# One more round between the residual and the second product of the Newton step, and three more instructions that the modulation sums stand behind

## The chip, the cores and the metric

The kernel runs on one core of one Trainium2 chip. The metric is device time in microseconds (us) of one execution. A core has TensorE (PE in the rows; PEld are its weight loads), VectorE (DVE), ScalarE (ACT), GpSimd (POOL) and SyncE (SP, which here issues nearly all DMAs). Each engine takes its instructions in the order in which they stand in the program, and waits for the others by semaphores.

## The reference

One layer of a diffusion backbone over 256 context and 256 latent tokens, model width 2048. What matters here is the RWKV-7 part, 16 heads of width 64, in both directions of time, first over the context, then over the latent tokens:

```python
def wkv_scan(r, w, k, v, kk, a, s0, reverse):
    def step(s, inp):
        r_t, w_t, k_t, v_t, kk_t, a_t = inp
        sa = jnp.einsum('bhij,bhj->bhi', s, -kk_t)
        s = (s * w_t[:, :, None, :] + sa[..., None] * (kk_t * a_t)[:, :, None, :]
             + v_t[..., None] * k_t[:, :, None, :])
        return s, jnp.einsum('bhij,bhj->bhi', s, r_t)
...
yx_rw, _ = rwkv_mix(rwkv_streams(conv3(px[..., :RW_COLS], rw_shift[i]), *rw_args), s_ctx, *out_args)
yx = jnp.concatenate([yx_rw.astype(px.dtype), short_conv_mix(px, conv_w[i], grid_conv3),
                      fourier_mix(px)], axis=-1) @ w_out[i]
x = x + ga1 * yx
x = x + ga2 * ffn(modulate(rms_norm(x, norm_ffn[i]), sh2, sc2), w_gate[i], w_up[i], w_down[i])
```

The modulation vectors (`ga1`, `sh2`, `sc2`, `ga2`) are sums over 2048 rows of a weight matrix, weighted by `silu(c)`.

## The kernel before

The program has three stages. The first makes the modulated inputs and a part of the projections. The second, the recurrence, holds everything between the projections and the FFN, and the third is the FFN.

**The recurrence** handles 16 states one after another: state 0 to 7 are the eight pairs of heads over the context, 8 to 15 the same pairs over the latent tokens. The tokens of a state are cut into 4 chunks of 64. Four kinds of Python generators work on a state: `rw_prep` makes its operands, two `rw_inverse` (one for each direction of time) invert the 64 by 64 triangular matrices of the chunks, and `rw_scan` runs over the chunks. `recurrence()` goes round by round: in every round each live generator emits its instructions up to its next `yield`, and yields an estimate of the TensorE time of what it emitted. A second stream, `fillers()`, holds all other TensorE work of this stage (projections, the Fourier part, the first part of the output projection). After the generators of a round, `tick` draws fillers until their estimates reach what is left of the round's budget: 2.2 (context) or 2.1 (latent) less what the generators have yielded, at least 0.65. TensorE's order is this order of the code (`manual_schedule`). The other engines' orders are made by a list scheduler when the program is built.

The fillers stop at two places. The second of three groups of the output projection waits until the first four pairs of heads are normed, and from its 9th column block on (`HOLD`) until the last state is done.

**The inverse** (`rw_inverse`) takes a mask step (`de`), five doubling steps in 16 bits (`sx`, `de`), and then one Newton step in 32 bits: a first product (TensorE, `iv<-d,ga`), the residual (VectorE, `idm`, one buffer for both directions), a second product (TensorE, `iv<-e,idm`), and the sum that refines the inverse (VectorE, `e`).

**The modulation sums** (`modvecs`) are 192 VectorE instructions of 128x512 (`macc<-wm`), each on a weight block that has just been loaded. 0.9 of them are drawn per round. `issue_after(self.lastv.ins)` places a sum behind the instruction that `lastv` names on VectorE, which is set in the doubling steps and in the scan.

Of the kernel before, what the change touches and what calls it, by code (L numbers as in the profile page):

```python
# [14 lines left out]
ALU = mybir.AluOpType  # L15
# [185 lines left out]
class Builder:  # L201
# [26 lines left out]
    def cst(self, name, i=0, n=None, rows=slice(0, P)):  # L228
        s, e = CC.at[name]
        return self.consts[rows, s + i:(e if n is None else s + i + n)]  # L230
# [503 lines left out]
    def rw_inverse(self, st, d):  # L734

        nc, mp, cst = self.nc, self.mp, self.cst
        V, S, G, T = nc.vector, nc.scalar, nc.gpsimd, self.t
        while len(st["GA"]) <= d or self.inverted[d] < st["n"]:
            yield 0.0
        ga = st["GA"][d]  # L740
        msk = lambda l: self.bc4(self.m16[:, 6 * d + l])
        quads = [(c, h) for c in range(NC) for h in range(2)]

        im = T(mp, [P, NC, C], F16, f"im{d}")
        for h in range(2):
            (G, V)[h].tensor_tensor(im[HV[h]], ga[h][HV[h]], self.bc4(cst("i64", rows=HV[h])), op=ALU.add)  # L746
        for h in range(2):
            G.tensor_tensor(ga[h][HV[h]], ga[h][HV[h]], self.bc4(cst("i64", rows=HV[h])), op=ALU.add)
        yield 0.0
        pq = T(self.iv, [P, NC, C], F32, f"iv{d}")  # L750
        for c, h in quads:
            self.mm(pq[HV[h], c], im[HV[h], c], self.i16[HV[h]], True, True)

        xe = T(mp, [P, 2, NC, C], F16, f"de{d}")
        V.tensor_tensor(xe[:, 0], pq, msk(0), op=ALU.mult)
        V.tensor_tensor(xe[:, 1], im, self.bc4(self.m16[:, 12 + d]), op=ALU.mult)
        yield 0.12
        sx = T(mp, [P, NC, C], F16, f"sx{d}")
        for l in range(1, 6):
            pd = T(self.iv, [P, 2, NC, C], F32, f"iv{d}")  # L760
            for c, h in quads:
                self.mm(pd[HV[h], 0, c], im[HV[h], c], xe[HV[h], 0, c], True, True)
            self.lastv = V.tensor_tensor(sx, pd[:, 0], msk(l), op=ALU.mult)
            yield 0.12
            for c, h in quads:
                self.mm(pd[HV[h], 1, c], sx[HV[h], c], xe[HV[h], 1, c], True, True)
            for c, h in quads:
                self.mm(pd[HV[h], 0, c], xe[HV[h], 1, c], sx[HV[h], c], True, True)
            if l < 5:
                S.copy(xe, pd)  # L770
            else:
                d32 = T(mp, [P, NC, C], F32, "d32")
                e32 = T(mp, [P, NC, C], F32, f"e32{d}", 2)
                S.copy(d32, pd[:, 0])
                S.copy(e32, pd[:, 1])
            yield 0.34
        pr = T(self.iv, [P, 2, NC, C], F32, f"iv{d}")
        for c, h in quads:
            self.mm(pr[HV[h], 0, c], ga[h][HV[h], c], d32[HV[h], c], True, True)
        r = T(mp, [P, NC, C], F32, "idm")  # L780
        V.tensor_tensor(r, self.bc4(cst("i64")), pr[:, 0], op=ALU.subtract)
        yield 0.6
        for c, h in quads:
            self.mm(pr[HV[h], 1, c], r[HV[h], c], e32[HV[h], c], True, True)
        V.tensor_tensor(e32, e32, pr[:, 1], op=ALU.add)
        st["E"][d] = e32
        self.inverted[d] += 1
        yield 0.6

    def rw_scan(self, st):  # L790

# [455 lines left out]
```

## Time and profile before

| | |
|---|---|
| time, three runs | 1812.42, 1812.53, 1805.78 us (median 1812.42) |
| profiled execution: time | 1805.89 us |
| profiled execution: span from first to last instruction | 1804.1 us |
| mean granted TensorE clock | 0.976 of full speed |
| recurrence in this execution | about 232 to 1036 us |
| TensorE / VectorE busy in the span | 94% / 58% |

Busy time is the time in which an engine has an instruction under way. Matmuls overlap, so that eight of them listed with 0.28 us each can take 0.12 us each from start to start. The span is the profiled execution from its first to its last instruction; the execution's own time is 1.8 us longer.

### The profile page before, as it was taken

To read this page: it belongs to the slowest core of one execution; us is meant where nothing else is said; L and a number is where in the kernel's file an instruction comes from. 1 tells how busy PE (TensorE), PEld (TensorE's weight loads), DVE (VectorE), ACT (ScalarE), POOL (GpSimd) and SP (SyncE) were. 2 spreads that over 40 slices of the span, in tenths; PEclk is the share of its full clock that TensorE was granted. 3 is DMA by queue.
4 is the path that set the end of the run, shared out by engine and by line. 5 is a ranking of instruction groups with operands and counts; after the bars stand their busy time and mean duration, and the time that the engine had idled before them with its cause. 6 is when DMAs were issued, how large, how long until landed. Compare 5 with 4: busy or idle time off the path is not lost.

```text
span 1804.1 us, 47455 instructions
## 1 busy us (share of the span) xinstructions
PE 1698.8 (94%) x19960; PEld 1561.3 (87%) x19960; DVE 1053.4 (58%) x1851; ACT 828.0 (46%) x1577; POOL 747.2 (41%) x650
## 2 busy tenths in 40 slices
PE   7999999988999899899988979999999999999996
PEld 3888988887888787787876779999999999999996
DVE  4444357777678777768875697555555444333333
ACT  2223455555655555444553444444444444444442
POOL 1224454455666554455652452232322323323332
PEclk9999999999999999899998989999999999999998
DMA  9992233455455443544542257777777566665654
GB/s 359 344 332 87 87 103 120 143 157 155 155 164 164 143 141 115 158 129 121 155 124 60 80 165 245 240 242 234 237 230 231 188 200 188 191 190 184 189 185 136
DMA packets 139237, 318.92 MB, mean 177 GB/s; under 512 B 14224, under 2 KB 40464, under 8 KB 139024
## 3 DMA queue, kind: packets, MB, share of 16 engines
q1 hardware_dynamic: 137936, 314.84, 54.5%
q8 instruction: 156, 2.56, 0.6%
q10 hardware_dynamic: 1088, 1.05, 0.2%
q14 instruction: 57, 0.47, 0.1%
HBM read 313.74 MB, written 2.10 MB: 175 GB/s over the span
## 4 chain that ended last, share of the span: by engine, by line
PE 77%; DVE 13%; ACT 4%; issue 3%; DMA 2%; POOL 1%; SPq 0%; DVEq 0%; ACTq 0%; POOLq 0%
PE gu L233 25%; PE pj L233 17%; PE dn L233 13%; PE pacc L233 4%; PE pp L233 4%; PE iv L233 4%; PE st L233 3%; PE acc L233 3%; DVE macc L1096 3%; PE pmod L233 2%; DVE bk L645 1%; DVE XL L1184 1%; DMA wm<-wma 1%; DVE im L746 1%; DVE HL L1155 1%
## 5 line engine op out<-in xcount | busy, mean ns | idle before, releaser
L269 POOL TENSOR_TENSOR wlo<-w,whi 128x512 fp32r<-128x512 f32 (+2 forms) x309 | 517.0, 1676 | 747.7 <-ACT whi L266 724.1
L266 ACT CAST whi<-w 128x1024 fp32r<-128x1024 f32 (+2 forms) x472 | 401.3, 851 | 552.5 <-PE gu L233 200.9
L233 PE MATMUL gu<-XH,whi 128*128 128x256 f32 (+1 forms) x1408 | 392.9, 279 | 4.5 <-ACT whi L266 4.0
L233 PE MATMUL gu<-XH,wlo 128*128 128x256 f32 (+1 forms) x1408 | 391.3, 279 | 2.1 <-POOL wlo L269 1.3
L269 DVE TENSOR_TENSOR wlo<-w,whi 128x1024 fp32r<-128x1024 f32 (+1 forms) x175 | 205.7, 1176 | 312.4 <-ACT whi L266 312.4
L233 PE MATMUL gu<-XL,whi 128*128 128x256 f32 x1344 | 372.6, 278 | 0.1
L233 PE MATMUL pj<-XH,whi 128*128 128x256 f32 x1016 | 290.1, 314 | 3.1 <-DVE XL L1028 2.3
L233 PEld LDWEIGHTS gu<-XH,whi 128*128 128x128 f32 x1408 | 266.1, 189 | 5.8 <-ACT whi L266 4.8
L233 PEld LDWEIGHTS gu<-XH,wlo 128*128 128x128 f32 x1408 | 265.5, 189 | 2.8 <-POOL wlo L269 1.7
L233 PE MATMUL pj<-XL,whi 128*128 128x256 f32 x1016 | 259.6, 284 | 0.6 <-DVE XL L269 0.6
L233 PE MATMUL pj<-XH,wlo 128*128 128x256 f32 x1016 | 259.6, 284 | 0.0
L233 PEld LDWEIGHTS gu<-XL,whi 128*128 128x128 f32 x1344 | 253.9, 189 | 0.3 <-DVE XL L1184 0.3
L233 PEld LDWEIGHTS pj<-XH,whi 128*128 128x128 f32 x1016 | 183.1, 192 | 18.3 <-issue 1.8
L233 PE MATMUL dn<-HL,whi 128*128 128x256 f32 x704 | 196.0, 278 | 0.0
L233 PE MATMUL dn<-HH,wlo 128*128 128x256 f32 x704 | 194.4, 276 | 0.0
L233 PE MATMUL dn<-HH,whi 128*128 128x256 f32 x704 | 194.3, 276 | 0.0
L233 PEld LDWEIGHTS pj<-XL,whi 128*128 128x128 f32 x1016 | 183.8, 193 | 2.4 <-issue 0.9
L233 PEld LDWEIGHTS pj<-XH,wlo 128*128 128x128 f32 x1016 | 183.0, 193 | 2.6 <-POOL whi L268 1.7
L1096 DVE SCALAR_TENSOR_TENSOR macc<-wm,sc,macc 128x512 f32<-128x512 f32 x180 | 164.6, 914 | 1.8 <-DMA wm<-wmb 1.1
L233 PEld LDWEIGHTS dn<-HL,whi 128*128 128x128 f32 x704 | 132.1, 188 | 1.4
L233 PEld LDWEIGHTS dn<-HH,wlo 128*128 128x128 f32 x704 | 132.2, 188 | 0.0
L233 PEld LDWEIGHTS dn<-HH,whi 128*128 128x128 f32 x704 | 132.1, 188 | 0.0
(302 smaller groups left out, 2774.4 us busy)
## 6 DMA issues: line engine op xcount, KB each, us to landing
w<-wgu SPq DMA_DIRECT2D x176, 512.0 KB, 4.7
wm<-wmb SPq DMA_DIRECT2D x192, 256.0 KB, 3.2
w<-wdn SPq DMA_DIRECT2D x80, 512.0 KB, 4.4
w<-wib SPq DMA_DIRECT2D x148, 256.0 KB, 3.4
wm<-wma SPq DMA_DIRECT2D x64, 512.0 KB, 7.3
XH<-wmb SPq DMA_DIRECT2D x64, 256.0 KB, 4.8
w<-wout SPq DMA_DIRECT2D x48, 256.0 KB, 3.0
wa<-wia SPq DMA_DIRECT2D x16, 416.0 KB, 5.2
```

The lines of the kernel that those rows point to most:

```text
L233: self.last = self.nc.tensor.matmul(out, lhsT=lhsT, rhs=rhs, start=start, stop=stop)
L266: he.copy(hi, src)
L269: le.tensor_tensor(lo, src, hi.bitcast(F32), op=ALU.subtract)
L645: V.tensor_tensor(bk[:, :, i], ch(f), ch(pi), op=ALU.mult)
L746: (G, V)[h].tensor_tensor(im[HV[h]], ga[h][HV[h]], self.bc4(cst("i64", rows=HV[h])), op=ALU.add)
L1096: V.scalar_tensor_tensor(acc, w, self.sc[:, k, 1:2], acc, op0=ALU.mult, op1=ALU.add)
L1155: V.scalar_tensor_tensor(ul[:, k, :L], X1[:, k], self.mod[:, 2, k:k + 1], uh[:, k, :L].bitcast(F32), op0=ALU.mult, op1=ALU.subtract)
L1184: V.scalar_tensor_tensor(XL[:, k], xn, bias, XH[:, k].bitcast(F32), op0=ALU.add, op1=ALU.subtract)
```

## The change

In `rw_inverse` the mask, the residual and the sum that refines the inverse are noted as `lastv` too, so that modulation sums that are emitted after them stand behind them on VectorE. The generator yields once more between the residual and the second product, so the second product comes one round later. The yields of the Newton step name 0.3, 0.0 and 0.3 in place of 0.6 and 0.6, so for each of the 32 inversions the budgets leave 0.6 more to the fillers.

```diff
--- before.py
+++ after.py
@@ -752,7 +752,7 @@
             self.mm(pq[HV[h], c], im[HV[h], c], self.i16[HV[h]], True, True)
 
         xe = T(mp, [P, 2, NC, C], F16, f"de{d}")
-        V.tensor_tensor(xe[:, 0], pq, msk(0), op=ALU.mult)
+        self.lastv = V.tensor_tensor(xe[:, 0], pq, msk(0), op=ALU.mult)
         V.tensor_tensor(xe[:, 1], im, self.bc4(self.m16[:, 12 + d]), op=ALU.mult)
         yield 0.12
         sx = T(mp, [P, NC, C], F16, f"sx{d}")
@@ -778,14 +778,15 @@
         for c, h in quads:
             self.mm(pr[HV[h], 0, c], ga[h][HV[h], c], d32[HV[h], c], True, True)
         r = T(mp, [P, NC, C], F32, "idm")
-        V.tensor_tensor(r, self.bc4(cst("i64")), pr[:, 0], op=ALU.subtract)
-        yield 0.6
+        self.lastv = V.tensor_tensor(r, self.bc4(cst("i64")), pr[:, 0], op=ALU.subtract)
+        yield 0.3
+        yield 0.0
         for c, h in quads:
             self.mm(pr[HV[h], 1, c], r[HV[h], c], e32[HV[h], c], True, True)
-        V.tensor_tensor(e32, e32, pr[:, 1], op=ALU.add)
+        self.lastv = V.tensor_tensor(e32, e32, pr[:, 1], op=ALU.add)
         st["E"][d] = e32
         self.inverted[d] += 1
-        yield 0.6
+        yield 0.3
 
     def rw_scan(self, st):
```

Lines from 783 on have one number more in the changed program.

TensorE at the Newton steps of state 0; `iv<-e,idm` are second products, `iv<-d,ga` a first product, `pj<-X..,w..` fillers. Before, from the last fillers ahead of the second product of the first direction (the rows `idm_3283`) to the second product of the other direction (`idm_3338`):

```order
L233 MATMUL pj_2999<-XH_4_62,wlo_3261 128x256
L233 MATMUL pj_2999<-XH_5_63,wlo_3261 128x256
L233 MATMUL iv_456_3274<-e_436_3192,idm_3283 64x64 x8
L233 MATMUL iv_461_3329<-d_458_3301,ga_374_2652 64x64
L233 MATMUL iv_461_3329<-d_458_3301,ga_375_2654 64x64
...
L233 MATMUL pj_2999<-XH_5_63,wlo_3261 128x256
L233 MATMUL pj_2999<-XH_4_62,whi_3347 128x256
...
L233 MATMUL pj_2999<-XH_5_63,wlo_3348 128x256
L233 MATMUL iv_461_3329<-e_459_3302,idm_3338 64x64 x8
```

and with the change, from the same fillers on:

```order
L233 MATMUL pj_2999<-XH_5_63,wlo_3261 128x256
L233 MATMUL iv_461_3320<-d_458_3301,ga_374_2652 64x64
L233 MATMUL iv_461_3320<-d_458_3301,ga_375_2654 64x64
...
L233 MATMUL pj_2999<-XH_5_63,wlo_3261 128x256
L233 MATMUL pj_2999<-XH_4_62,whi_3338 128x256
...
L233 MATMUL pj_2999<-XH_5_63,wlo_3339 128x256
L233 MATMUL iv_456_3274<-e_436_3192,idm_3283 64x64 x8
L233 MATMUL pp_3367<-aq_3226,bk_3228 128x64
L233 MATMUL pp_3368<-aq_3226,bk_3228 128x64
...
L233 MATMUL pj_2999<-XH_4_62,whi_3338 128x256
L233 MATMUL iv_461_3320<-e_459_3302,idm_3329 64x64 x8
```

The first product of the second direction now comes ahead of the second product of the first, and three groups of fillers (18 matmuls) stand between these two where none stood.

VectorE at the same place; `bk`, `aq` and `sm` belong to `rw_prep`, `macc` is a modulation sum. Before:

```order
L717 SCALAR_TENSOR_TENSOR sm_3164<-consts_60,tw_3159 128x256
L645 TENSOR_TENSOR bk_3228<-f_3229,sm_3117 128x4x64
L645 TENSOR_TENSOR bk_3228<-f_3233,sm_3117 128x4x64
L1096 SCALAR_TENSOR_TENSOR macc_3125<-wm_3358,sc_121,macc_3125 128x512
L781 TENSOR_TENSOR idm_3283<-consts_60,iv_456_3274 128x256
L635 TENSOR_TENSOR aq_3242<-px_3237,kk_3099 128x4x64
L1096 SCALAR_TENSOR_TENSOR macc_3125<-wm_3390,sc_121,macc_3125 128x512
L785 TENSOR_TENSOR e_436_3192<-e_436_3192,iv_456_3274 128x256
L1096 SCALAR_TENSOR_TENSOR macc_3125<-wm_3424,sc_121,macc_3125 128x512
L645 TENSOR_TENSOR bk_3244<-f_3245,sm_3164 128x4x64
L781 TENSOR_TENSOR idm_3338<-consts_60,iv_461_3329 128x256
```

and with the change:

```order
L717 SCALAR_TENSOR_TENSOR sm_3164<-consts_60,tw_3159 128x256
L645 TENSOR_TENSOR bk_3228<-f_3229,sm_3117 128x4x64
L645 TENSOR_TENSOR bk_3228<-f_3233,sm_3117 128x4x64
L781 TENSOR_TENSOR idm_3283<-consts_60,iv_456_3274 128x256
L1097 SCALAR_TENSOR_TENSOR macc_3125<-wm_3317,sc_121,macc_3125 128x512
L635 TENSOR_TENSOR aq_3242<-px_3237,kk_3099 128x4x64
L645 TENSOR_TENSOR bk_3244<-f_3245,sm_3164 128x4x64
L645 TENSOR_TENSOR bk_3244<-f_3249,sm_3164 128x4x64
L781 TENSOR_TENSOR idm_3329<-consts_60,iv_461_3320 128x256
L1097 SCALAR_TENSOR_TENSOR macc_3125<-wm_3355,sc_121,macc_3125 128x512
L786 TENSOR_TENSOR e_436_3192<-e_436_3192,iv_456_3274 128x256
```

One modulation sum fewer stands ahead of the first residual (`idm_3283`), and the second residual now stands ahead of the sum that refines the first inverse (`e_436`). The second residual takes the buffer that the first one's second product reads.

TensorE at the Newton steps of state 14, late in the recurrence; `pp<-aq,bk` belongs to `rw_prep` of state 15. Before:

```order
L233 MATMUL pj_15655<-XL_1955_12644,whi_15657 128x256
L233 MATMUL pj_15655<-XH_1954_12643,wlo_15658 128x256
L233 MATMUL iv_2456_15668<-e_2435_15585,idm_15677 64x64 x8
L233 MATMUL iv_2461_15720<-d_2458_15695,ga_2342_14948 64x64
L233 MATMUL iv_2461_15720<-d_2458_15695,ga_2343_14951 64x64
...
L233 MATMUL pj_15732<-XH_1954_12643,whi_15734 128x256
L233 MATMUL pj_15732<-XL_1955_12644,whi_15734 128x256
L233 MATMUL pj_15732<-XH_1954_12643,wlo_15735 128x256
L233 MATMUL iv_2461_15720<-e_2459_15696,idm_15729 64x64 x8
L233 MATMUL pp_15761<-aq_15619,bk_15622 128x128
```

and with the change:

```order
L233 MATMUL iv_2494_15856<-d_2476_15789,ga_2377_15147 64x64
L233 MATMUL iv_2494_15856<-d_2476_15789,ga_2378_15150 64x64
...
L233 MATMUL iv_2478_15793<-sx_2423_15364,de_2413_15298 64x64
L233 MATMUL iv_2499_15890<-d_2496_15883,ga_2392_15198 64x64
L233 MATMUL iv_2499_15890<-d_2496_15883,ga_2393_15201 64x64
...
L233 MATMUL iv_2494_15856<-e_2477_15790,idm_15865 64x64 x8
L233 MATMUL pp_15914<-aq_15824,bk_15827 128x128
L233 MATMUL pp_15915<-aq_15824,bk_15827 128x128
...
L233 MATMUL iv_2499_15890<-e_2497_15884,idm_15899 64x64 x8
```

Between the products of the two directions no filler is left here. Counted over TensorE's whole order, 6 to 12 fillers stood between the first and the second product of the first direction in states 0 to 7, and 24 to 33 stand there now. 1761 filler matmuls stood between the first direction's second products of state 0 and state 12, and 1932 stand there now; from state 12 to state 15 there were 381 (165 of them from state 13 to 14 and 96 from state 14 to 15), and 192 are left (132 and none). The rounds of the recurrence number 280 before and 288 now; those in which no filler was to be had 28 before and 59 now.

## Rows read from the trace of the kernel before

**Rows 1.** The page: busy time of the engines, share of the span, instructions.
```profile
PE 1698.8 (94%) x19960; PEld 1561.3 (87%) x19960; DVE 1053.4 (58%) x1851; ACT 828.0 (46%) x1577; POOL 747.2 (41%) x650
```

**Rows 2.** Stretches: us, busy us of PE, PEld, DVE, ACT, POOL, then PE's clock, DMA.
```profile
263.00:444.00 181.00, 166.30 (x2731) 150.26 (x2733) 134.41 (x274) 104.79 (x251) 96.46 (x107) 0.99 0.47 143
444.00:625.00 181.00, 167.24 (x2677) 150.64 (x2676) 134.96 (x271) 108.40 (x255) 111.43 (x119) 0.96 0.51 157
625.00:827.00 202.00, 182.72 (x2853) 155.54 (x2851) 146.53 (x305) 105.43 (x254) 107.37 (x127) 0.96 0.44 136
827.00:877.00 50.00, 46.78 (x714) 39.09 (x712) 42.91 (x93) 24.44 (x57) 25.74 (x33) 1.00 0.47 138
877.00:929.00 52.00, 48.43 (x770) 42.62 (x765) 37.57 (x84) 28.91 (x69) 34.38 (x34) 0.97 0.43 130
929.00:968.00 39.00, 34.37 (x649) 30.31 (x646) 28.32 (x64) 14.75 (x35) 17.26 (x17) 1.00 0.44 130
968.00:992.00 24.00, 17.99 (x146) 11.04 (x145) 12.06 (x32) 4.63 (x12) 2.15 (x5) 0.67 0.02 6
```

**Rows 3.** TensorE's waits, 263 to 969 us: us in total, times, longest.
```profile
PE iv L233 <- DVE idm L781: 25.9, 15, 4.2
PE iv L233 <- DVE de L755: 5.9, 6, 2.2
PE pp L672 <- DVE mq L665: 4.7, 3, 1.6
...
PE st L233 <- DVE w L847: 3.0, 3, 2.1
PE iv L233 <- DVE sx L763: 3.0, 3, 1.3
PE pp L233 <- DVE mq L665: 2.9, 8, 0.9
```

**Rows 4.** TensorE in time at two waits: start, us, instruction, [idle before it <- releaser].
```profile
437.44 0.68 PE L233 MATMUL iv<-d,ga 64*64 64x64 f32 x16
...
438.30 0.39 PE L233 MATMUL pj<-XH,whi 128*128 128x256 f32 x1
...
439.67 0.28 PE L233 MATMUL pj<-XH,wlo 128*128 128x256 f32 x1
443.12 0.68 PE L233 MATMUL iv<-e,idm 64*64 64x64 f32 x16 [3.17 <-DVE idm L781]
...
933.21 0.68 PE L233 MATMUL iv<-e,idm 64*64 64x64 f32 x16 [2.10 <-DVE idm L781]
```

**Rows 5.** VectorE in time at the first of these waits.
```profile
438.07 1.22 DVE L1096 SCALAR_TENSOR_TENSOR macc<-wm,sc,macc 128x512 f32<-128x512 f32 x1
439.21 1.86 DVE L645 TENSOR_TENSOR bk<-f,sm 128x256 f32<-128x256 f32 x2
440.99 1.75 DVE L1096 SCALAR_TENSOR_TENSOR macc<-wm,sc,macc 128x512 f32<-128x512 f32 x1
442.66 0.41 DVE L781 TENSOR_TENSOR idm<-consts,iv 128x256 f32<-128x256 f32 x1
```

**Rows 6.** Short stretches, columns as in rows 2.
```profile
395.90:399.30 3.40, 3.40 (x19) 3.18 (x18) 0.29 (x1) 0.62 (x1) 0.36 (x1) 0.50 0.13 42
...
624.60:628.00 3.40, 3.40 (x38) 3.10 (x38) 2.03 (x3) 0.07 (x1) 3.40 (x4) 0.50 0.57 175
971.40:976.20 4.80, 1.18 (x30) 0.86 (x26) 3.92 (x8) 0.67 (x2) 0.00 (x0) 1.00 0.01 3
976.20:996.70 20.50, 18.11 (x96) 12.50 (x92) 7.79 (x24) 3.11 (x10) 3.68 (x6) 0.50 0.03 6
```

**Rows 7.** The modulation sums (tile macc), 263 to 969 us: who waited for them.
```profile
L1096 DVE SCALAR_TENSOR_TENSOR macc<-wm,sc,macc x176: 731/750/1864, 263.8 to 956.3; 128x512 f32<-128x512 f32 x176
...
  DVE mod L1110: 11.5, 9
```

**Rows 8.** TensorE by line, 240 to 1100 us: first matmuls of a filler's weight block.
```profile
L233 PE MATMUL pj<-XH,whi 128*128 128x256 f32 x808 | 247.3, 321 | 3.1 <-DVE XL L1028 2.3 <-ACT whi L266 0.6
```

## The prediction

> **What bounds the kernel now.** I read four views, in this order. The page says that TensorE is busy for 94% of the span and VectorE for 58% [rows 1]; over a span of stages with different limits this only says where to look. The table by stretches shows the stage that the change touches: from 263 to 968 us TensorE is busy 645.8 of 705 us, summed over six rows. So 59 us of the recurrence are idle on TensorE, and a change of order can win little more than that. VectorE is busy 134 of 181 us early and 42.9 of 50 us in the worst late stretch [rows 2]. The view of waits says who ended TensorE's idle time there: 25.9 us, in 15 of the 32 inversions, were ended by the residual `idm`. No other releaser takes more than 5.9 us [rows 3].
>
> The timelines of both engines show why. At 437.44 us the first product runs, then only 12 fillers stand before the second product. These are through at about 439.8 us, 1.5 us for the twelve, so 0.12 us each. TensorE then sits 3.17 us [rows 4]. VectorE meanwhile does not touch the residual, which could have started at 438.1: it works through two modulation sums and two `bk` that stand ahead of it, from 438.07 to 442.7 us [rows 5]. The wait is a matter of the queue, and the residual itself takes 0.41 us. In the other direction it is the same (2.10 us at 933.21) [rows 4].
>
> A stall has an aftermath. After four of the long ones the granted clock is at half level, 1.2 in place of 2.4 GHz, for some 3.4 us, with TensorE busy throughout. The same is seen on a larger scale at 971 us, where TensorE had worked 1.18 of 4.8 us, and 20.5 us at half level followed [rows 6].
>
> **The change, part by part.** The sum is made against the profiled execution's own 1805.9 us, which equals the lowest of the three runs and lies 6.5 us under their median.
>
> *The wait itself.* In the first direction 24 to 33 fillers stand between the two products in the context states, where 6 to 12 stood. At 0.12 us the 15 to 24 more are 1.8 to 2.9 us [rows 4], besides the other direction's first product; that nearly covers the 3.17 us of the stall shown, and covers shorter ones wholly. In the second direction the residual must wait until the first direction's second product has read the buffer, so there is still just one round for it. But it stands right behind the work of two rounds, ahead of the sum `e`, and where fillers are to be had 12 or more and `rw_prep`'s matmuls lie behind it. One modulation sum of some 0.9 us less stands ahead of many residuals, too. Bounds: nothing, or all 25.9 us [rows 3]. I take 22, since the late states lose the cover.
>
> *The clock.* Four stretches of 3.4 us at half level [rows 6] cost half their length, 6.8 us. Bounds 0 and 6.8; with 22 of 25.9 us of the stalls gone I take 5.8.
>
> *What comes late next.* TensorE's stall was also time in which VectorE caught up. VectorE's other results already make TensorE wait 5.9 (`de`), 7.6 (`mq`), 3.0 (`w`) and 3.0 us (`sx`) [rows 3]. A backlog that is not waited for at the second product meets one of these. Bounds: nothing, since VectorE has 47 idle us of the first 181 [rows 2], and all 22 us. I take 5, a quarter more of these 19.5.
>
> *Fillers drawn earlier.* The new yields leave 0.6 more per inversion to the fillers. 171 matmuls more are spent between states 0 and 12, and 189 fewer are left from state 12 to 15, none at all in the last of these. Their own time only moves: 189 by 0.12 us is 22.7 us. What counts is whether the late stretch, 827 to 968 us, shrinks by as much. TensorE is busy there for 129.6 of 141 us, VectorE for 108.8 [rows 2], and VectorE's work stays. Without the fillers TensorE has 106.9 us, less than VectorE. So VectorE sets the end. If it gets to the 86% of its best stretch now (42.91 of 50), the stretch takes 126.5 us, 14.5 less, so 8.2 of the 22.7 us are lost. If it gets to 92%, nothing is lost; if it stays at its 77%, all 22.7. I take 8.
>
> *More of the low clock.* [...] Bounds: nothing, and 10 us if another 20 us run so. I take 2, since from 929 to 968 us with 88% the clock stayed at 1.00 [rows 2].
>
> *The sums that stand back.* Modulation sums are moved behind masks, residuals and refined inverses. Nobody on TensorE waited for them; the 11.5 us that VectorE itself waited after them are for TensorE's products of the sums [rows 7]. Cost nothing, covered by the two rounds between the last sum and its product. Without that cover one sum, 0.75 us by its median, for each of 12 groups: 9 us. The mask's own 5.9 us of waits [rows 3] could shrink for the same reason; I leave them, since the sums ahead of a mask were mostly emitted before it. Weight loads lie behind the sums' loads on SyncE's queue, and these wait for a sum to free a buffer. But TensorE waited 0.6 us in all for a filler's upper half of the weights [rows 8], so a round of delay there is hidden.
>
> *Eight more rounds.* The scan of a state comes a round later. Where fillers fill the rounds that costs nothing; where not, it is part of the late stretch.
>
> Sum: 1805.9 - 22 - 5.8 + 5 + 8 + 2 = 1793.1 us, 12.8 us or 0.7% less.
>
> **A rule against it.** The rows of the late stretch show two engines near their limits at once, TensorE 129.6 and VectorE 108.8 of 141 us [rows 2], because fillers are mixed into VectorE's work. The Trainium skill, "Perfetto Trace Analysis", section "Optimization Strategy", says that where the most-contended engine changes over time, performance may be improved by interleaving the regimes. The change does the reverse late in the recurrence. The skill gives no figure. If the rule decides, the stretch keeps its length and the time is that of the second rival; by the first terms alone it would be 1783.1.
>
> **The rivals.** *The wait comes back elsewhere: about 1806.* VectorE takes its queue in order. The second direction's residual now waits at its head until the other direction's second product is done, and everything behind it waits too. Between the two residuals stand some 2 us of VectorE work (a sum, an `aq`, two `bk`), and TensorE needs 3.4 to 4.5 us until that product is done (24 to 33 fillers at 0.12 us, and a first product of some 0.5). The hold is 1 us or more; 1.2 us in 16 states is 19 us. If TensorE pays them at the next VectorE results, the 5 above become 19, and 1793.1 + 14 = 1807. For it: VectorE is busy for three quarters. Against: its idle quarter, and that the residual does not come to the head at once.
>
> *Slower: the late stretch runs dry, about 1815.* If VectorE stays at 77% there, 22.7 in place of 8 are lost, and with 10 in place of 2 for the clock the time is 1793.1 + 14.7 + 8 = 1815.8. It turns to slower than before at 23 us lost there (1805.9 - 1783.1), VectorE's part and the clock's together. For it: 31 more rounds without fillers, and what the clock did after 971 us. Against: from 929 to 968 us, with no more than 96 fillers (11.5 us), TensorE was still busy for 88% [rows 2].
>
> *More: about 1777.* All 25.9 + 6.8 us are won, nothing is given back, and the late stretch loses 4: 1777.2.
>
> That the change does not do what it says is excluded by the order of the instructions.
>
> **How the numbers follow.** Chances: the forecast 0.5, the wait that comes back 0.27, slower 0.13, more 0.1. A measurement of this kernel can tell about 0.5%, 9 us, from no change. The forecast's own range is 1780 to 1802; some 0.42 of its 0.5 lie beyond 9 us of gain, 0.08 within. The wait that comes back is 0.22 within, 0.02 faster, 0.03 slower; the dry stretch 0.11 slower and 0.02 within; the last is faster. Together: faster 0.54, same 0.32, slower 0.14. Two of three runs before lay 6.5 us above the profiled one. Whether the new runs fall on the one level or the other the profile doesn't say; I put the predicted time between the two: 1812.4 less 12.8 is 1799.6, 1793.1 is the lower, so 1797. The range takes in both levels and reaches from 1778 (the last rival) to 1819 (the slow one, on the upper level in part).
>
> **What the profile of the changed kernel would show.** The waits ended by `idm` fall from 25.9 us to under 6. Waits ended by `de`, `mq`, `w`, `sx` and `rhs` rise by some 5 us. The stretch from the first to the last second product keeps its length or gets up to 20 us shorter, with the gain before state 12 and a part given back behind it. VectorE is busy for over 83% between states 12 and 15, and TensorE waits there for it. The stretches at half clock before state 12 get fewer. I am wrong if VectorE's waits take the place of `idm` early, or if the stretch behind state 12 gets hardly shorter than now.

## The result, and the profile after

The changed kernel takes 1821.18 us (median of 19 runs, 1810.81 to 1831.13), the kernel before 1809.86 us (median of 19): a ratio of 1.0057, 95% interval 1.0039 to 1.0074. It is slower by 10 us; 13 us of gain were forecast. The profiled execution of the changed kernel is the lowest of its 19, 1810.81 us, 4.9 us above the one of before, so its trace shows about half of the loss. The ratios below leave out four runs (one of e1, two of e5, one of e7) that took over 1.5% longer than the fastest run of the same kernel.

The page of the changed kernel (busy time, share of the span, instructions) reads as before [rows 1]:

```profile
PE 1704.3 (94%) x19960; PEld 1563.6 (86%) x19960; DVE 1049.2 (58%) x1851; ACT 827.5 (46%) x1577; POOL 744.2 (41%) x650
```

The waits of TensorE after the change, from the first direction's second product of state 0 to that of state 15:

```profile
PE pp L233 <- DVE mq L665: 8.0, 12, 2.6
PE iv L233 <- DVE sx L763: 6.7, 10, 2.3
PE st L233 <- DVE rhs L824: 6.1, 4, 2.6
PE iv L233 <- ACT de L770: 6.0, 12, 2.3
PE iv L233 <- ACT e L775: 4.8, 8, 1.7
PE st L233 <- ACT UV L835: 4.2, 9, 0.8
PE pp L672 <- DVE mq L665: 4.1, 4, 1.5
PE iv L233 <- DVE idm L781: 3.1, 4, 1.9
PE acc L233 <- DVE XH L883: 2.9, 1, 2.9
```

The waits for `idm` fell from 25.9 us [rows 3] to 3.1. But `mq` rose from 7.6 to 12.1, `sx` from 3.0 to 6.7, and ScalarE's `e` takes 4.8 us. To see what is left of the gain, the stretches are cut at the first direction's second products of states 0, 8, 12 and 15. Before (length, busy time of PE, PEld, DVE, ACT, POOL, PE's clock, DMA):

```profile
262.90:624.60 361.70, 333.24 (x5396) 300.60 (x5396) 269.07 (x544) 213.30 (x506) 207.59 (x226) 0.98 0.49 150
624.60:826.60 202.00, 182.72 (x2843) 155.54 (x2843) 146.53 (x305) 105.43 (x254) 107.37 (x127) 0.96 0.44 137
826.60:968.40 141.80, 130.38 (x2127) 112.48 (x2127) 109.25 (x239) 68.51 (x161) 77.78 (x83) 0.99 0.44 132
```

and after:

```profile
267.20:640.80 373.60, 351.83 (x5533) 317.38 (x5532) 272.49 (x549) 217.84 (x514) 221.96 (x235) 0.98 0.52 155
640.80:845.60 204.80, 184.35 (x2885) 156.69 (x2884) 147.00 (x309) 106.86 (x255) 112.71 (x128) 0.97 0.46 142
845.60:974.10 128.50, 111.39 (x1934) 92.75 (x1930) 97.54 (x227) 59.83 (x145) 52.41 (x66) 0.93 0.35 103
```

Length less PE's busy time is TensorE's idle time: 28.5 + 19.3 + 11.4 = 59.2 us before, 21.8 + 20.4 + 17.1 = 59.3 us after. All 22.8 us won at `idm` were given back within the same stage. The late stretch got 13.3 us shorter, the first one 11.9 and the middle one 2.8 us longer, together 1.4 us longer; 4.3 us lie ahead of the first cut, where one more round with its fillers now stands. And the late stretch runs at a clock of 0.93, where it ran at 0.99. Over the whole span the mean granted clock is 0.973 (0.976 before), which is 0.003 of 1809 us or 5.4 us of TensorE's time, beside the 4.9 us by which this execution is longer. In the timed runs the median clock is 0.967, that of before 0.972 in the runs beside the first experiments: 9 us, beside a measured loss of 10. That the clock alone makes the loss is not shown by this.

At the place of [rows 4, 5] the step does what it was forecast to do. TensorE at the Newton step of state 4 after the change (start, us, instruction):

```profile
450.89 0.68 PE L233 MATMUL iv<-d,ga 64*64 64x64 f32 x16
451.50 0.38 PE L233 MATMUL pj<-XH,whi 128*128 128x256 f32 x1
...
453.55 0.28 PE L233 MATMUL pj<-XH,wlo 128*128 128x256 f32 x1
453.76 0.68 PE L233 MATMUL iv<-e,idm 64*64 64x64 f32 x16
...
456.99 0.68 PE L233 MATMUL iv<-e,idm 64*64 64x64 f32 x16
```

and VectorE there:

```profile
449.13 0.41 DVE L781 TENSOR_TENSOR idm<-consts,iv 128x256 f32<-128x256 f32 x1
449.46 1.45 DVE L1097 SCALAR_TENSOR_TENSOR macc<-wm,sc,macc 128x512 f32<-128x512 f32 x1
452.82 0.48 DVE L326 SCALAR_TENSOR_TENSOR sg<-pj,vecs,sg 128x255 f32<-128x255 f32 x1 [1.90 <-ACT sg L325]
453.34 0.48 DVE L328 SCALAR_TENSOR_TENSOR sg<-pj,vecs,sg 128x255 f32<-128x255 f32 x1
454.49 0.42 DVE L781 TENSOR_TENSOR idm<-consts,iv 128x256 f32<-128x256 f32 x1 [0.67 <-PE iv L233]
454.82 0.41 DVE L786 TENSOR_TENSOR e<-e,iv 128x256 f32<-128x256 f32 x1
```

The first residual is done at 449.54, 4.2 us before the second product reads it; no wait is left. But the second direction's residual, whose operand is there at 451.57, starts at 454.49, when the first direction's second product is through, 2.9 us later. For most of this time VectorE waits for and does two `sg` of the fillers that stand ahead; for the last 0.67 us it has nothing else to do, and the single buffer holds it.

### The profile page after: what moved, and what is told of

It is laid out like the page before. It is cut to its first block, busy times and chain, and to the rows that moved or that the text cites. A ratio compares the mean times of both kernels' runs of the same rounds, so it can differ in the third digit from the quotient of the medians.

```text
span 1809.0 us, 47450 instructions
## 1 busy us (share of the span) xinstructions
PE 1704.3 (94%) x19960; PEld 1563.6 (86%) x19960; DVE 1049.2 (58%) x1851; ACT 827.5 (46%) x1577; POOL 744.2 (41%) x650
## 4 chain that ended last, share of the span: by engine, by line
PE 57%; DVE 9%; ACT 4%; POOL 2%; DMA 2%; issue 2%; DVEq 0%; ACTq 0%; POOLq 0%; SPq 0%
PE gu L233 24%; PE dn L233 13%; PE pj L233 9%; PE iv L233 3%; PE acc L233 3%; PE pp L233 2%; PE st L233 2%; DVE macc L1097 1%; POOL wlo L269 1%; DMA w<-wib 1%; DVE XL L1185 1%; ACT whi L266 1%; DMA w<-wgu 1%; DVE bk L645 1%; DVE im L746 1%
## 5 line engine op out<-in xcount | busy, mean ns | idle before, releaser
L233 PE MATMUL pj<-XH,whi 128*128 128x256 f32 x1016 | 284.8, 308 | 2.0 <-DVE XL L1029 2.0
L1097 DVE SCALAR_TENSOR_TENSOR macc<-wm,sc,macc 128x512 f32<-128x512 f32 x180 | 169.0, 939 | 0.3
```

Of the source, the lines that this page charges most:

```text
L233: self.last = self.nc.tensor.matmul(out, lhsT=lhsT, rhs=rhs, start=start, stop=stop)
L1097: V.scalar_tensor_tensor(acc, w, self.sc[:, k, 1:2], acc, op0=ALU.mult, op1=ALU.add)
```

## The experiments

Four suspects: the **fillers** drawn earlier (smaller yields, and a round more that draws fillers too), the **buffer** that holds the second residual, the **notes** that place the modulation sums, and the further **round** itself. Each ratio is to runs of the kernel before on the same chip.

| kernel | rounds without fillers | ratio, 95% interval | idle, three stretches (us) |
|---|---|---|---|
| before | 28 | 1 | 28.5, 19.3, 11.4 |
| whole change | 59 | 1.0057 (1.0039 to 1.0074) | 21.8, 20.4, 17.1 |
| e1 yields alone | 44 | 1.0004 (0.9975 to 1.0034) | 28.3, 16.3, 15.2 |
| e2 round alone | 44 | 0.9983 (0.9963 to 1.0003) | 25.1, 15.9, 11.6 |
| e3 notes alone | 28 | 0.9895 (0.9863 to 0.9927) | 18.1, 16.6, 8.7 |
| e4 whole, two buffers | 59 | 1.0009 (0.9989 to 1.0030) | 22.6, 18.2, 15.5 |
| e5 whole, fillers kept | 30 | 0.9920 (0.9890 to 0.9950) | 18.8, 17.9, 8.4 |
| e6 yields and notes | 44 | 0.9957 (0.9936 to 0.9978) | 16.8, 16.7, 12.9 |
| e7 fillers kept, two buffers | 30 | 0.9883 (0.9855 to 0.9910) | 17.5, 17.7, 8.0 |
| e8 notes, two buffers | 28 | 0.9918 (0.9890 to 0.9946) | 17.2, 16.7, 8.9 |
| e9 note on the residual | 28 | 0.9905 (0.9874 to 0.9937) | 19.8, 16.0, 10.4 |
| e10 notes on mask and inverse | 28 | 0.9898 (0.9871 to 0.9925) | 20.4, 16.3, 9.9 |
| e11 notes, fillers later | 21 | 0.9905 (0.9878 to 0.9931) | 25.4, 16.3, 9.2 |
| e12 as e7, fillers later | 21 | 0.9857 (0.9829 to 0.9886) | 16.5, 20.9, 7.9 |
| e13 as e4, early in context only | 49 | 0.9958 (0.9943 to 0.9973) | 23.5, 13.5, 12.9 |
| e14 as e4, early in latent only | 39 | 0.9891 (0.9862 to 0.9920) | 17.7, 17.0, 9.2 |
| e15 whole, no notes | 59 | 1.0066 (1.0046 to 1.0086) | 28.8, 17.8, 16.4 |
| e16 whole, old yields | 44 | 0.9975 (0.9956 to 0.9993) | 23.1, 18.7, 11.7 |

**e1, the yields alone.**

```diff
-        yield 0.6
+        yield 0.3
         for c, h in quads:
...
-        yield 0.6
+        yield 0.3
```

> The kernel before with the smaller yields alone (0.3 and 0.3 in place of 0.6 and 0.6), no further round and no new notes. In the order of the code the rounds without fillers go from 28 to 44, half of the way to the 59 of the whole change. If the early spending of fillers costs the time (the late stretch runs dry): about 5 us slower, ratio 1.003, with the loss behind state 12. If the buffer that holds back the second residual, the notes or the round do it: no loss, and a gain of up to 5 us, because 2 to 3 more fillers stand in each round and the waits for idm, 25.9 us before, shrink somewhat; ratio 0.997 to 1.000.

1.0004: neither the loss of the one theory nor a clear gain. Idle time moved behind state 12 (11.4 to 15.2 us) and left the middle stretch.

**e2, the round alone.**

```diff
         yield 0.6
+        yield 0.0
         for c, h in quads:
```

> The kernel before with the further round alone (yields 0.6, 0.0, 0.6). Rounds without fillers 44, as with the smaller yields alone. The waits for idm should fall from 25.9 us to under 5 in every theory. If the early spending of fillers costs the time: some 5 us slower less what the waits give, ratio 0.998 to 1.003. If the second residual, held at the head of VectorE's queue by the single buffer, gives the wait back at VectorE's other results (rhs, mq, sx, UV, e): about 10 us slower, ratio 1.005, with these waits as high as after the whole change. If the notes do it: 10 us or more faster, ratio 0.994 or less.

0.9983, in the range expected of the early fillers. The waits for `idm` fell only to 18.8 us, not under 5 as every theory had it. 16.8 of them are in the second direction, whose residual still has sums and other work ahead of it.

**e3, the notes alone.**

```diff
-        V.tensor_tensor(xe[:, 0], pq, msk(0), op=ALU.mult)
+        self.lastv = V.tensor_tensor(xe[:, 0], pq, msk(0), op=ALU.mult)
...
-        V.tensor_tensor(r, self.bc4(cst("i64")), pr[:, 0], op=ALU.subtract)
+        self.lastv = V.tensor_tensor(r, self.bc4(cst("i64")), pr[:, 0], op=ALU.subtract)
...
-        V.tensor_tensor(e32, e32, pr[:, 1], op=ALU.add)
+        self.lastv = V.tensor_tensor(e32, e32, pr[:, 1], op=ALU.add)
```

> The kernel before with the three notes for the modulation sums alone; rounds and fillers as before. If the notes place the sums badly: about 10 us slower, ratio 1.005. In the other theories nothing, ratio 0.998 to 1.002, and the waits for idm shrink by some 5 us at most since a sum less stands ahead of many residuals.

0.9895: one per cent faster, 19 us, which no theory had. The waits for `idm` of this kernel:

```profile
PE iv L233 <- DVE idm L781: 9.2, 9, 2.7
```

and its three stretches:

```profile
263.30:611.20 347.90, 329.79 (x5397) 297.39 (x5396) 264.43 (x543) 211.94 (x503) 206.94 (x225) 0.99 0.50 155
611.20:812.60 201.40, 184.76 (x2842) 157.85 (x2842) 144.64 (x306) 105.48 (x258) 108.61 (x127) 0.94 0.45 139
812.60:954.30 141.70, 132.98 (x2127) 114.29 (x2127) 109.05 (x240) 68.62 (x162) 77.67 (x83) 0.96 0.43 132
```

The number of TensorE's instructions in each stretch is that of before; the first got 13.8 us shorter, and the idle time fell by 15.8 us. So the three notes win more than was forecast for the whole, and the whole change is 1.6% behind the notes alone.

**e4, the whole change with two buffers.**

```diff
-        r = T(mp, [P, NC, C], F32, "idm")
+        r = T(mp, [P, NC, C], F32, "idm", 2)
```

> The whole change, with two buffers for the residual in place of one, so that the second direction's residual need not wait for the first direction's second product. The order of TensorE is that of the whole change. If the hold at the head of VectorE's queue gives the wait back: the loss of 10 us goes and some 10 us are won, ratio to the kernel before 0.995, and the waits for rhs, mq, sx, UV and e (39 us with the whole change) come down by 10 or more. If the early spending of fillers, the notes or the round itself cost the time: as the whole change, ratio 1.005 to 1.007, with these waits unchanged.

1.0009, between the two. The hold is gone, as VectorE at the same place shows:

```profile
452.61 0.41 DVE L781 TENSOR_TENSOR idm<-consts,iv 128x256 f32<-128x256 f32 x1
452.94 1.45 DVE L1097 SCALAR_TENSOR_TENSOR macc<-wm,sc,macc 128x512 f32<-128x512 f32 x1
455.10 0.42 DVE L781 TENSOR_TENSOR idm<-consts,iv 128x256 f32<-128x256 f32 x1 [0.71 <-PE iv L233]
```

The second residual starts at 455.10, behind its own first product; the first direction's second product follows only at 457.24. The two `sg` now stand behind it, so the second buffer also changes VectorE's order. The buffer accounts for about 0.5%, hold and order together; the waits for `rhs`, `mq`, `sx`, `UV` and `e` hardly changed, so most has another cause. The stretches of this kernel:

```profile
266.80:643.80 377.00, 354.39 (x5534) 319.49 (x5533) 272.08 (x550) 217.99 (x514) 223.35 (x235) 0.97 0.50 154
643.80:847.00 203.20, 185.05 (x2885) 158.63 (x2884) 148.85 (x309) 106.74 (x255) 113.53 (x128) 0.97 0.46 143
847.00:971.90 124.90, 109.38 (x1930) 90.76 (x1930) 95.50 (x227) 59.77 (x145) 51.98 (x66) 0.96 0.36 106
```

**e5, the whole change with the fillers spent as before.**

```diff
-        yield 0.3
+        yield 0.9
         yield 0.0
...
-        yield 0.3
+        yield 0.9
```

> The whole change, but with yields of 0.9, 0.0 and 0.9, so that the fillers are spent as before: 30 rounds without fillers (28 before, 59 with the whole change) and the same sum of fillers up to state 12. One buffer for the residual. What is to be shared out: notes alone 0.9895, whole change 1.0057, whole change with two buffers 1.0009. If the early spending of fillers takes the gain: 0.994 (the notes' 0.9895 and some 0.005 for the single buffer), and from state 12 to 15 the stretch is 142 us long as before. If the round itself takes it (refined inverses one round later, a scan one round later): 1.004 or more, with the waits for rhs, UV, e and mq as high as with the whole change.

0.9920, as the fillers' theory said (0.994); the late stretch is 138.0 us. Round, notes and buffer are those of the whole change, so the two numbers of the yields turn 1.0057 into 0.9920.

**e6, yields and notes** (e1 and e3 together).

```diff
...
-        V.tensor_tensor(r, self.bc4(cst("i64")), pr[:, 0], op=ALU.subtract)
-        yield 0.6
+        self.lastv = V.tensor_tensor(r, self.bc4(cst("i64")), pr[:, 0], op=ALU.subtract)
+        yield 0.3
...
```

> Notes and smaller yields (0.3 and 0.3), no further round. 44 rounds without fillers. If the early spending of fillers takes the notes' gain: about half of it, ratio 0.995. If the round itself does it: as the notes alone, ratio 0.989 to 0.991, since the yields alone measured 1.0004.

0.9957, over half of the notes' gain lost, as the fillers' theory said. It needs no further round.

**e7, fillers spent as before, and two buffers** (e4 and e5 together).

```diff
+        r = T(mp, [P, NC, C], F32, "idm", 2)
...
+        yield 0.9
         yield 0.0
...
```

> Round and notes with the fillers spent as before (yields 0.9, 0.0, 0.9) and two buffers for the residual: all suspected costs but the round itself are away. If early spending and the single buffer are the whole loss: as the notes alone or better, ratio 0.985 to 0.990. If the round itself costs: 1.000 or so, as the whole change with two buffers. The waits for idm are about nothing in both.

0.9883, no slower than the notes alone: the round itself costs nothing that shows. Against e4 (1.0009) only the yields differ, 1.26% or 23 us. The stretches of e7:

```profile
265.50:609.50 344.00, 326.52 (x5380) 294.40 (x5379) 273.96 (x545) 210.28 (x499) 206.21 (x222) 1.00 0.53 158
609.50:809.90 200.40, 182.71 (x2859) 154.62 (x2857) 150.49 (x312) 105.25 (x255) 111.34 (x126) 0.97 0.47 141
809.90:949.40 139.50, 131.49 (x2115) 113.06 (x2114) 103.15 (x230) 68.77 (x161) 75.47 (x82) 0.97 0.43 125
```

From e7 to e4, 153 matmuls of the fillers' tile `pj` more lie in the first stretch (1330 and 1483) and 187 fewer in the last (395 and 208), 18 and 22 us at 0.12 us. The first stretch becomes 33.0 us longer, the last only 14.6 us shorter. The 33.0 us are 18 of moved work, 5.1 of idle time (17.5 and 22.6) and some 11 of clock: 1.00 against 0.97. Over the three stretches the idle time is 43.2 us in e7 and 56.3 in e4.

**e8, notes and two buffers, no round.**

```diff
...
+        r = T(mp, [P, NC, C], F32, "idm", 2)
+        self.lastv = V.tensor_tensor(r, self.bc4(cst("i64")), pr[:, 0], op=ALU.subtract)
         yield 0.6
...
```

> The notes and two buffers, no further round, yields as before. Without the round the second direction's residual stands right behind the first direction's second product, so the single buffer should hold nothing. Both theories: as the notes alone, 0.987 to 0.991. If it is faster than that by 0.3% or more, the buffer costs even where no round is added.

0.9918, as the notes alone within the intervals: without the round the single buffer costs nothing that shows.

**e9 and e10, the notes apart**: that on the residual alone, and those on mask and inverse alone.

```diff
+        self.lastv = V.tensor_tensor(r, self.bc4(cst("i64")), pr[:, 0], op=ALU.subtract)
```

> The kernel before with the note on the residual alone. If the notes win because the sums of the round go behind the residual that TensorE waits for: nearly all of what the three notes win, ratio 0.990 to 0.993, with idm waits near 9 us. If it is the mask or the refined inverse: 0.998 to 1.002, idm waits near 26.

```diff
+        self.lastv = V.tensor_tensor(xe[:, 0], pq, msk(0), op=ALU.mult)
...
+        self.lastv = V.tensor_tensor(e32, e32, pr[:, 1], op=ALU.add)
```

> The kernel before with the notes on the mask and on the refined inverse alone. If the residual's note is what counts: 0.997 to 1.002, with idm waits of 20 us or more. If the other two count: 0.990 to 0.993.

0.9905 and 0.9898: each half wins what all three win, which neither theory had. The waits for `idm` are 9.2 us in e9, 17.3 in e10. So the notes' gain is not only that the residual comes sooner. The waits for the mask (`de` of L755), 5.9 us before [rows 3], show another part: they are 3.9 us in e9, and none are left in e10 or with all three notes (e3).

```profile
PE iv L233 <- DVE de L755: 3.9, 4, 1.8
```

Both waits together fell by 18.7 us in e9, 14.5 in e10 and 22.6 in e3, and the idle time of the three stretches by 13.0, 12.6 and 15.8. So a part of what is won is given back elsewhere, and the two halves don't add.

**e11, notes with larger yields.**

```diff
-        yield 0.6
+        yield 0.9
...
-        yield 0.6
+        yield 0.9
```

> The three notes with larger yields (0.9 and 0.9 in place of 0.6 and 0.6), no further round: fillers are spent later than before, 21 rounds without fillers in place of 28. If the time turns on when the fillers run out: a gain on the notes' 0.9895, ratio 0.985 to 0.989, with less idle time behind state 12. If less cover early costs as much as more cover late gives: 0.989 to 0.993, with idm waits above 9 us.

0.9905: no gain on the notes. The idle time of the first stretch rises from 18.1 to 25.4 us, most likely since cover is now missing there.

**e12, as e7 with still larger yields.**

```diff
+        yield 1.2
         yield 0.0
...
+        yield 1.2
```

> Round, notes, two buffers, and fillers spent later than before (yields 1.2, 0.0 and 1.2; 21 rounds without fillers, against 59 with the whole change). With the fillers spent as before the ratio was 0.988. If spending fillers later gives more: 0.983 to 0.987. If before's own spending is about right: 0.987 to 0.992. In both the waits for idm stay at about nothing.

0.9857, 1785.89 us: the best version found, faster than both kernels; its interval overlaps that of e7. The median granted clock of its runs is 0.9855 (0.977 in e7, 0.967 in the whole change), and the late stretch runs at 1.00:

```profile
809.20:950.80 141.60, 133.71 (x2159) 115.09 (x2158) 105.01 (x236) 70.86 (x164) 81.23 (x86) 1.00 0.43 131
```

**e13 and e14, early spending in one half of the states.**

```diff
+        yield 0.3 if st["n"] < NP else 0.9
         yield 0.0
...
+        yield 0.3 if st["n"] < NP else 0.9
```

> Round, notes and two buffers, with the yields 0.3, 0.0 and 0.3 in the context states alone and 0.9, 0.0 and 0.9 in the latent states. 49 rounds without fillers (30 with 0.9 throughout, ratio 0.9883; 59 with 0.3 throughout, 1.0009). If the loss goes with the number of rounds without fillers: 19 of 29 of the way, 0.9965. If it arises where the fillers are spent, in the context states: the whole of it, 1.000. If it arises only in the latent states' own larger draws: 0.988 to 0.990.

(e14: `>=` for `<`.)

> The same with the yields the other way round: 0.9, 0.0 and 0.9 in the context states, 0.3, 0.0 and 0.3 in the latent ones. 39 rounds without fillers. If the loss goes with the number of rounds without fillers: 9 of 29 of the way, 0.992. If it arises in the context states: 0.988. If in the latent states: 0.997 to 1.001.

0.9958 and 0.9891. With 30, 39, 49 and 59 rounds without fillers the ratios are 0.9883, 0.9891, 0.9958 and 1.0009, in that order, though not quite in proportion: 9 and 19 of 29 steps give 0.992 and 0.9965. The first and last stretch of e13:

```profile
265.80:642.30 376.50, 352.97 (x5526) 318.43 (x5526) 272.30 (x549) 217.28 (x513) 223.97 (x235) 0.97 0.50 154
...
840.50:966.90 126.40, 113.49 (x1951) 95.39 (x1953) 95.20 (x224) 60.62 (x147) 57.27 (x68) 0.94 0.37 111
```

The first stretch is that of e4, 32.5 us above e7, and the last gives back 13.1 us. What is spent early in the context states is not got back late. Of the 1.26% between e7 and e4, early spending in the context states alone makes 0.75%, in the latent states alone 0.08%.

**e15, the whole change without the notes.**

```diff
...
-        self.lastv = V.tensor_tensor(r, self.bc4(cst("i64")), pr[:, 0], op=ALU.subtract)
+        V.tensor_tensor(r, self.bc4(cst("i64")), pr[:, 0], op=ALU.subtract)
         yield 0.3
         yield 0.0
...
```

> The whole change without the three notes (one buffer, yields 0.3, 0.0 and 0.3). If the notes still win something in the whole change: slower than it, 1.010 or more. If the round and the fillers already cover what the notes would win: as the whole change, 1.004 to 1.008. If the notes harm there: 1.000 or less.

1.0066, as the whole change within the intervals: what wins 1% alone wins next to nothing here.

**e16, the whole change with the old yields.**

```diff
-        yield 0.3
+        yield 0.6
         yield 0.0
...
-        yield 0.3
+        yield 0.6
```

> Round and notes with the yields 0.6, 0.0 and 0.6, one buffer: 44 rounds without fillers, between the 30 of the yields 0.9 (ratio 0.992) and the 59 of the whole change (1.0057). If the loss goes with the number of rounds without fillers: 0.999. If it comes only with the last of them: 0.992 to 0.995.

0.9975, between the 0.9920 of 30 rounds and the 1.0057 of 59, as the count had it (0.999).

## Why the prediction was wrong, step by step

**The wait itself (-22): right.** 22.8 us of the 25.9 went, and the order did it as described. It took the round and the smaller yields together: 18.8 us are left with the round alone (e2), 24.5 with the yields alone (e1), 6.4 with both and no notes (e15).

**What comes late next (+5): too small by half even where the fillers are kept.** With the fillers spent as before and the single buffer (e5) the three stretches idle for 45.1 us. That is 14.1 below before's 59.2, where 24.7 us of waits for `idm` went, so 10.6 us came back. In the whole change all came back.

**Fillers drawn earlier (+8) and more of the low clock late (+2): the steps that failed.** They were 10 us together. Measured by the yields alone, they are 1.0009 less 0.9883, about 23 us, between e7 and e4, and 1.0057 less 0.9920, about 25 us, with one buffer. The step that failed is that the fillers' "own time only moves" between the stretches: against e7, 18 us of it cost the first stretch of e4 33.0 us, and 22 us less gave the last one 14.6. The mechanism of the late stretch was wrong too. It said that VectorE sets the end of the late stretch and that its work stays there. VectorE's share stayed at 76%, near the 77% of the worse bound, but its work fell with the fillers, from 109.25 to 97.54 us, and the stretch shrank by 13.3 us, near the 14.5 forecast. Of the 17.1 us for which TensorE is idle there now, 7.1 end with a result of the doubling steps (`de`, `sx`), which have few or no fillers between them, and 3.3 with `mq`. The waits from state 12 to 15 after the change:

```profile
PE iv L233 <- ACT de L770: 3.9, 6, 2.3
PE pp L233 <- DVE mq L665: 3.3, 5, 1.5
PE iv L233 <- DVE sx L763: 3.2, 3, 2.3
```

Before, `de` of ScalarE and `sx` were not among the waits of this stretch. The late clock, +2 in the sum, cost some 7.6 us: length by one less the clock is 1.4 us before and 9.0 after. And the prediction looked for the price in the late stretch alone. The larger part of it lies in the context states, where more TensorE work was taken as merely moved; there it brought idle time and half clock with it (e7 against e4, e13).

A part of this can be read from the traces, though no run tests it: fillers that are drawn sooner meet weights that have not landed. ScalarE makes a filler's upper weights (`whi`) from a block that a DMA brings. For these loads it waited 26.0 us in the first stretch of the whole change. The same before, in e7 and in e4:

```profile
ACT whi L266 <- DMA w<-wib: 0.3, 1, 0.3
...
ACT whi L266 <- DMA w<-wib: 7.6, 5, 3.6
...
ACT whi L266 <- DMA w<-wib: 24.1, 13, 4.1
```

The longest of them in e4, on ScalarE, VectorE and TensorE, and TensorE's stretch behind it (columns as in the stretches above):

```profile
598.50 0.62 ACT L266 CAST whi<-w 128x512 fp32r<-128x512 f32 x1 [4.09 <-DMA w<-wib]
599.02 0.50 ACT L325 ACTIVATE XL<-XL,vecs 128x256 f32<-128x256 f32 x1
...
599.55 1.18 DVE L326 SCALAR_TENSOR_TENSOR XL<-XL,vecs 128x252 f32<-128x252 f32 x1 [3.04 <-ACT XL L325]
...
600.99 0.41 DVE L665 TENSOR_TENSOR mq<-pp,consts 128x256 f32<-128x256 f32 x1
...
601.54 0.76 PE L233 MATMUL pp<-aq,bk 64*128 64x128 f32 x2 [2.86 <-DVE mq L665]
...
601.50:610.80 9.30, 8.69 (x55) 8.04 (x56) 6.00 (x16) 2.05 (x5) 4.74 (x7) 0.50 0.17 55
```

A convolution of the fillers (`XL`) stands behind the late weights on ScalarE, its second part ahead of `mq` on VectorE, and TensorE sits idle for 2.86 us and then runs at the half level for 9.3. The wait and half of the 9.3 us are some 7.5 us of the 23. The whole change, e13 and e15 have the same wait for `mq` (2.62, 2.92 and 2.75 us); in e7 and e14 TensorE does not wait for `mq` in the first stretch.

**The clock (-5.8): wrong in sign.** Four half-clock stretches were to go with the stalls. Over the three stretches the clock's shortfall, length by one less the clock, is 16.7 us before and 22.6 after (the column has two digits); in the first stretch, where the stalls went, it is 7.2 and 7.5. In the late part the clock falls after a milder lull than at 971 us before [rows 6]. Here TensorE was busy for 2.50 and 1.82 of 3.4 us, and then came the half level (0.50):

```profile
943.70:947.10 3.40, 2.50 (x52) 2.06 (x48) 3.28 (x8) 0.00 (x0) 0.00 (x0) 1.00 0.33 99
947.10:950.50 3.40, 1.82 (x24) 1.46 (x24) 3.34 (x9) 0.00 (x0) 1.90 (x3) 0.88 0.51 148
950.50:953.90 3.40, 2.80 (x36) 2.50 (x38) 2.82 (x8) 1.17 (x2) 1.90 (x3) 0.50 0.29 82
```

**The sums that stand back (0): a gain was missed.** Notes alone win 1%. The prediction counted only the sum less ahead of the residual, inside the 22 us, and so gave the credit to the round. It left the mask's 5.9 us as they were, "since the sums ahead of a mask were mostly emitted before it"; with the mask's note they are gone (e3, e10). The two gains overlap and don't add: notes without round 0.9895, round and notes with the fillers kept 0.9883 to 0.9920, notes on top of round and early fillers nothing (e15).

**Eight more rounds (0): right** (e7).

**The rivals.** The *wait that comes back elsewhere* named the buffer rightly. The hold is in the trace, but its price is 0.5% or 9 us (1.0057 against e4's 1.0009) and 0.4% in the pair e5 and e7, whose intervals overlap; 14 more than the forecast was said. In the whole change VectorE is idle ahead of the residuals for 11.4 us in all, waiting for TensorE, and for 7.7 in e4; these 3.7 us more are less than the 9. The *dry late stretch* gave 1815.8 us; the forecast base of 1805.9 times 1.0057 is 1816.2. That the two agree is luck in good part: the rival took the whole price from the late stretch, which did shrink, and the larger part lies in the context states. The rule that was weighed against the change (the Trainium skill, "Perfetto Trace Analysis", section "Optimization Strategy": interleave regimes of different limits) goes with what was measured in its direction. The ratio rises as the fillers leave the late stretch (e7, e14, e13, e4); but that stretch did not keep its length, as was said of the rule.

**Open.** The smaller yields alone cost nothing (e1), and the first nine rounds without fillers hardly any (e14). So the price is not one per round, and it shows once the waits for `idm` are gone by other means. Whether weight loads that are issued sooner would win the price in the context states back was not tried, nor what makes the other falls of the clock there.

## What to carry to other kernels

Filler work is a stock. If a change makes an engine's wait shorter, check at once whether it also spends more of the stock per step, and hold the spending where it was while you test the step itself. Of a bundle of edits that attack one wait, take each alone first: here three notes won 1%, and the bundle lost 0.6%. Price a dry stretch by TensorE's idle time and by the clock that follows it, and price the stretch that receives the work as well as the one that loses it. See whether the loads of that work keep up when it is drawn sooner.

## What the runs showed of the hardware

The granted clock can fall without one long wait. From 943.7 to 950.5 us of the changed kernel TensorE was busy for 4.32 of 6.8 us, its two longest waits took 1.23 and 1.47 us (the second ends at 951.1), and from 950.5 us on the clock is at the half level. Over kernels with the same work the median clock of the runs ranged from 0.967 (the whole change) to 0.9855 (e12). Of 1800 us that is 33 us, beside 35 us between their medians (1821.18 and 1785.89). The clock is not the whole of it: in the two profiled executions, 20.3 us apart, it makes 14.4 us (0.973 and 0.981), and TensorE's idle time in the three stretches falls by 14.0 us, so that the two overlap. Among the runs of one kernel the time hardly follows the clock: of the 17 of the kernel before beside e9 to e12 (0.967 to 0.974) the longest, 1829.04 us, has the 0.974.
